# An encoder trunk on one core: the mLSTM recurrence's products in two groups a head, gate sums by transposes, and the order of the last output turns

## The chip, the cores and the metric

The kernel runs on one core of a Trainium2 chip. The metric is the device time of one execution in microseconds (us); less is better. Before the change it is 2804.45 us, the median of three runs from 2801.84 to 2805.65.

The engines' names in the profile: PE is TensorE (matrix products; PEld is its weight loads), DVE is VectorE, ACT is ScalarE, POOL is GpSimd, and SP is SyncE, which issues the DMAs. PSUM is the memory that PE writes its sums to. It has eight banks of 128 partitions x 512 float32 values, and the kernel hands them out one by one.

## What is computed

One layer of a hybrid encoder on 2048 tokens of width 1024, in float32. The part that the change touches is the mLSTM: 4 heads of 128 features, each with a 128 x 128 matrix memory that is carried from chunk to chunk. Cut to what matters (the input gate and forget gate come from eight columns of the input projection; `w`, `dw`, `s_prev` and `inter` are exponentials of gate sums):

```python
proj = rms_norm(x) @ w_in                        # q, k, v, mq, mk, mv, mo, i, f, ga, gm
att = chunk_band_attention(q, k, v, rel_bias)    # 8 heads, own chunk and 8 before it
# mLSTM, for each chunk and head:
c_loc = einsum('lv,lk->vk', w * v, k)
c_new = s_prev * c_prev + s_loc * c_loc          # state before the chunk: c_prev, n_prev
num = inter * (c_prev @ q) + (qk * dw) @ v
den = inter * (n_prev @ q) + sum(qk * dw)
hout = num / maximum(abs(den), exp(-m))
# then a norm for each head, gates, projections:
x = x + (sigmoid(ga) * (att @ w_att_proj) + sigmoid(gm) * (mlstm @ w_mlstm_proj)) @ w_out
x = x + square(relu(rms_norm(x) @ w_up)) @ w_down
out = rms_norm(x)
```

## The kernel before

The 2048 tokens are four blocks of 512. The kernel works on the mLSTM in chunks of 128 tokens, so a block has four chunks. Blocks 0 and 1 are worked one after the other with plain products; blocks 2 and 3 ("far") are taken together by a scheme of seven products in place of eight (`quad`, `quad_tok`, `down`), with intermediate tiles kept in HBM. Large products are made of three products of split operands (high by high, high by low, low by high): `mm3`, lines 531 to 533, and `quad`, line 616. They are the dense work, and the profile shows their 128x512 matmuls on those lines. Small products, the recurrence's and all transposes, are float32 without a split. The planner calls them full products and marks them "pe~"; the profile records each float32 product twice and each transpose once.

**The planner.** The program is a set of threads, Python generators that ask for an engine and a time ("pe~", 660) or for buffers ("get", a pool, how many). `Flow` plays them against a clock of its own when the kernel is built, and the order in which it grants the engines is the order of the instructions. Its latencies (LAT) and the times in the yields are estimates in the code. One thread, `dense`, issues the dense work and has the last priority; the threads of the attention, the recurrence and the evacuations put their PE steps between. A PE step of such a thread is placed SLACK (800 ns) after the time at which the planner expects it to be ready, so that PE finds it ready; NEAR (150) holds instead where PE is already at full products. SWITCH (85) is charged to the first product behind full ones that isn't full itself. A thread gets PSUM banks only if `want` banks less those that the dense work holds stay free for the dense work.

**The gates** (`gates`, from line 1354). The gate columns' product lands in a bank as 40 rows of 512 tokens, the low part's sums in rows 32 to 39 and the high part's in rows 0 to 7. ACT copies it to tmp. Four products (line 1368), one for 128 tokens each, with the 40 x 8 matrix sel, turn it and add the two parts. DVE adds the bias: in block 0 with a scale, four instructions (line 1374), in the others one (line 1378). `gates_rest` makes the exponentials of it.

**The recurrence** (`rec_head`, from line 1605). For each block and head: w gets the decay weights, kt the turned and weighted keys, then w the weighted scores. Then the loop over the four chunks takes one bank a chunk and puts three float32 products into it: scores by values (line 1654), weighted keys by values (1655), queries by the state cst (1656). DVE makes the next state (1659) from cst and the second product, and the next chunk's third product reads it. `rec_out` (from line 1711) scales the third product on ACT (1714), adds the first on DVE (1716), frees the bank, and sums squares (1720). Behind the loop, the head's output is normed, turned (1691) and multiplied by its output gate (1695). There are 4 blocks of 4 heads, so 64 rounds of the loop. In blocks 0 and 1 several heads are under way at once; in blocks 2 and 3 one at a time (N_REC).

**The end** (`final`). The norm of the last block needs a sum over the features of squares. `final1` squares each tile of features; the last one's square goes its own way (line 2310). `final_scale` adds them up with products by ones (lines 2393 and, for the last tile, 2400), DVE takes the means (2404) and POOL the root (2408). `final_out` turns the tiles (2426), four of 128x128 for each token tile t and half g of the features, scales them on ACT (2437) or DVE (2439) and stores 128 x 512 values (2443). A thread of it waits for its four tiles to be scaled before it turns them, and for the root before it scales.

Of the kernel before, what the change touches and what calls it, by code (L numbers as in the profile page):

```python
# [27 lines left out]
ALU = mybir.AluOpType  # L28

P = 128  # L30
# [4 lines left out]
NT = T // P  # L35
KT = D // P
AH, AD = 8, 64
MH = 4
# [57 lines left out]
class Flow:  # L96
# [141 lines left out]
class Layer:  # L238
# [1115 lines left out]
    def gates(self, b, bk, less=None):  # L1354
        fl, nc, B, sm = self.fl, self.nc, self.blk[b], self.sm
        V = nc.vector
        if b == 1:
            yield "wait", self.blk[0]["mix_ev"][4:]
        (tmp,) = yield "get", self.temp, 1
        yield "act", act_ns(512, True)  # L1360
        nc.scalar.copy(tmp[:40, :512], bk[:40])
        if less is not None:
            yield "dve", dve_ns(512)
            V.tensor_sub(tmp[:40, :512], tmp[:40, :512], less[:40])
            fl.put(self.banks, less)
        yield "pe~", 756
        for c in range(NT):
            nc.tensor.matmul(bk[:, c * 8:c * 8 + 8], tmp[:40, c * P:(c + 1) * P], self.sel[:40],
                             start=True, stop=True)
        gf = self.gf[b % 2]  # L1370
        if b == 0:
            for c in range(NT):
                yield "dve", 85
                V.scalar_tensor_tensor(gf[:, c], bk[:, c * 8:c * 8 + 8], self.rr["x"][:, c:c + 1],
                                       self.bif[:, c], op0=ALU.mult, op1=ALU.add)
        else:
            yield "dve", 85
            V.tensor_add(gf, bk[:, :32].rearrange("p (a b) -> p a b", a=NT), self.bif)
# [226 lines left out]
    def rec_head(self, b, h):  # L1605
# [42 lines left out]
        nev = [Event() for _ in range(NT)]  # L1648
        for c in range(NT):
            n = c * MH + h  # L1650
            sl = slice(c * P, (c + 1) * P)
            (bk,) = yield "get", self.banks, 1
            yield "pe~", 660
            mm(bk[:, 0:129], w[:, sl], mv[c], start=True, stop=True)  # L1654
            mm(bk[:, 130:259], kt[:, sl], mv[c], start=True, stop=True)  # L1655
            mm(bk[:, 260:389], q[:, sl], cst, start=True, stop=True)  # L1656
            fl.spawn(self.rec_out(n, bk, ndv[:, c], hs, c, nev[c]), 1)
            yield "dve", 265
            V.scalar_tensor_tensor(cst, cst, ex[:, 3, n:n + 1], bk[:, 130:259], op0=ALU.mult, op1=ALU.add)
        yield "wait", nev  # L1660
        den = ndv[:, :, 128]
        exh = ex[:, 0].rearrange("p (c m) -> p c m", c=NT)[:, :, h]
# [45 lines left out]
            fl.put(self.rec_room, 0)  # L1708
        fl.set(B["mix_ev"][4 + h])

    def rec_out(self, n, bk, nd, hs, c, ev):
        fl, nc = self.fl, self.nc
        yield "act", act_ns(129, True, 1)
        nc.scalar.mul(nd, bk[:, 260:389], self.ex[:, 1, n:n + 1])
        yield "dve", dve_ns(129)
        nc.vector.tensor_add(nd, bk[:, 0:129], nd)
        fl.put(self.banks, bk)
# [667 lines left out]
    def final_scale(self, s, h, slot, summed, ready):  # L2385
# [9 lines left out]
        if last:  # L2395
            fl.put(self.bias, slot)
            yield "wait", [self.last_ev]
            yield "pe~", 900
            for t in range(NT):
                nc.tensor.matmul(bk[:, 2 * t:2 * t + 2], self.sq_last[:, t * P:(t + 1) * P], self.ones,  # L2400
                                 start=False, stop=True, skip_group_check=True)
        r = self.rr[f"z{h}"]
        yield "dve", 75
        nc.vector.tensor_scalar(r, bk[:, :2 * NT].rearrange("p (t a) -> p t a", a=2)[:, :, 0], 1.0 / D, None,
# [15 lines left out]
    def final_out(self, s, h, t, g, scaled, ready, sent):  # L2420
        fl, nc = self.fl, self.nc
        yield "wait", scaled
        (bk,) = yield "get", self.banks, 1
        yield "pe~", 107 * 4
        for i in range(4):
# [8 lines left out]
        e = yield "act|dve", 650  # L2434
        r = self.rr[f"z{h}"][:, t:t + 1]
        if e == "act":
            nc.scalar.mul(o[:, :512], bk, r)
        else:
            nc.vector.tensor_scalar(o[:, :512], bk, r, None, op0=ALU.mult)
        fl.put(self.banks, bk)  # L2440
        row = (2 * s + h) * T + t * P
        yield "sp", 900, 2000
        nc.sync.dma_start(self.io["out"][row:row + P, g * 512:g * 512 + 512], o[:, :512])
        fl.put(pool, slot)
        fl.set(sent)

# [4 lines left out]
    def build(self):  # L2451
# [25 lines left out]
        self.last_ev, self.ev_late, self.ev_r, self.ev_gain, self.ev_const = (Event() for _ in range(5))  # L2477
# [129 lines left out]
```

## Time and profile before

| what | value |
|---|---|
| time, median of three runs | 2804.45 us |
| the profiled execution's own time | 2800.38 us |
| its span, first to last instruction | 2798.6 us |
| granted PE clock, mean | 0.999 |
| PE busy | 2776.0 us |
| DVE busy | 2069.1 us |
| ACT busy | 1563.4 us |
| HBM traffic | 437.46 MB read, 179.31 MB written |

How to read it: the profile is of one execution, with times from the start of the span. A row of the groups gives line, engine, operation, tiles (out<-in), shapes and count, then busy time and the mean ns of one, then the engine's idle time just before them and what ended it. A matmul's end is modelled, and matmuls overlap: the distance from one start to the next says what one costs. A row of the timeline has start, length, the instruction and how many were merged; the idle time before it stands in brackets. A row of the waits has who waited for whom, then us in total, times, and the longest. A row of the windows has the stretch, its length, the busy time of each engine that is named in its heading, and at the end the granted clock, the DMA engines' busy share and GB/s.

### The profile page before, as it was taken

The page shows a single profiled execution, that of the slowest core. Times are in us where ns is not written, and L with a number is a line of the kernel's source. Part 1 is how long each engine was busy: PE and PEld are TensorE (multiplying, and loading weights), DVE is VectorE, ACT ScalarE, POOL GpSimd, SP SyncE. Part 2 cuts the span into 40 slices and gives each one's busy share as a digit, 9 for nine tenths or more (in the row PEclk, how much of TensorE's full clock was granted, in tenths as well). Part 3 has the DMA queues.
Part 4 walks back from the last instruction along what each step waited for, and adds up shares of the span by engine and source line. Part 5 has one row for each costly group of instructions (what it writes and reads, how often), then busy time and mean ns, then how long its engine had stood idle before and what let it go on. Part 6 is the DMA issues. An engine that isn't in the chain of part 4 may idle for free.

```text
span 2798.6 us, 38177 instructions
## 1 busy us (share of the span) xinstructions
PE 2776.0 (99%) x13100; PEld 2300.7 (82%) x13100; DVE 2069.1 (74%) x3827; ACT 1563.4 (56%) x2707; POOL 50.5 (2%) x116
## 2 busy tenths in 40 slices
PE   9999999999999999999999999999999999999998
PEld 7888888888878888888888888888888888888887
DVE  7986489958885976875777888789877564457675
ACT  5774366755453544585555776466544665554443
POOL 0000000000000000000000000000000000000000
PEclk9999999999999999999999999999999999999999
DMA  6326742267845689657878876867777475677773
GB/s 223 102 90 211 266 147 90 97 209 240 268 154 201 230 289 311 218 199 256 305 286 296 279 242 210 254 193 231 236 253 238 171 255 206 208 268 263 266 260 130
DMA packets 283634, 619.33 MB, mean 221 GB/s; under 512 B 31536, under 2 KB 46000, under 8 KB 283440
## 3 DMA queue, kind: packets, MB, share of 16 engines
q1 hardware_dynamic: 283296, 616.88, 65.7%
q8 instruction: 103, 1.69, 0.2%
q14 instruction: 91, 0.75, 0.1%
q10 hardware_dynamic: 144, 0.01, 0.0%
HBM read 437.46 MB, written 179.31 MB: 220 GB/s over the span
## 4 chain that ended last, share of the span: by engine, by line
PE 90%; DVE 5%; issue 2%; ACT 2%; DMA 1%; POOL 0%; SPq 0%; POOLq 0%; DVEq 0%; ACTq 0%
PE bank L616 40%; PE bank L531 13%; PE bank L532 12%; PE bank L533 12%; PE bank L644 3%; PE bank L1272 2%; PE bank L1310 2%; PE bank L1344 2%; DVE wsp L472 1%; PE bank L1654 0%; PE bank L1636 0%; PE bank L1656 0%; PE bank L1655 0%; ACT wsp L470 0%; DVE r L1349 0%
## 5 line engine op out<-in xcount | busy, mean ns | idle before, releaser
L616 PE MATMUL bank<-r,wsp 128*128 128x512 f32 x5208 | 1188.6, 390 | 0.9 <-DVE r L1022 0.7
L616 PEld LDWEIGHTS bank<-r,wsp 128*128 128x128 f32 x5208 | 976.3, 188 | 208.4 <-issue 1.9
L472 DVE TENSOR_TENSOR wsp<-wraw,wsp 128x1024 fp32r<-128x1024 f32 x460 | 562.4, 1223 | 309.5 <-ACT wsp L470 301.0
L470 ACT CAST wsp<-wraw 128x1024 fp32r<-128x1024 f32 x460 | 483.0, 1050 | 493.6 <-PE bank L616 246.6
L531 PE MATMUL bank<-r,wsp 128*128 128x512 f32 x1600 | 636.0, 398 | 2.2 <-DVE ctx L1695 1.5
L532 PE MATMUL bank<-r,wsp 128*128 128x512 f32 x1600 | 625.2, 391 | 0.0
L533 PE MATMUL bank<-r,wsp 128*128 128x512 f32 x1600 | 624.8, 391 | 0.0
L533 PEld LDWEIGHTS bank<-r,wsp 128*128 128x128 f32 x1600 | 300.4, 188 | 64.2
L531 PEld LDWEIGHTS bank<-r,wsp 128*128 128x128 f32 x1600 | 300.6, 188 | 59.0 <-DVE ctx L1695 1.9
L532 PEld LDWEIGHTS bank<-r,wsp 128*128 128x128 f32 x1600 | 301.1, 188 | 55.2 <-DVE r L1294 0.8
L1848 DVE TENSOR_TENSOR ctx<-bank,ctx 128x512 f32<-128x512 f32 x174 | 119.4, 689 | 101.8 <-PE bank L616 101.7
L1020 DVE TENSOR_TENSOR r<-r 128x512 fp32r<-128x512 f32 x224 | 149.2, 688 | 61.1 <-ACT r L1015 60.1
L1015 ACT CAST r<-r 128x512 fp32r<-128x512 f32 x224 | 135.3, 621 | 94.2 <-DMA r<-u 91.1
L1840 ACT COPY ctx<-bank 128x512 f32<-128x512 f32 x174 | 100.9, 582 | 75.7 <-PE bank L616 67.7
L1325 ACT ACTIVATE sc<-sc,scs 128x640 f32<-128x640 f32 (+4 forms) x128 | 97.4, 761 | 62.4 <-DVE scs L1322 58.5
L1316 DVE CUSTOM_DVE_ANT_0 sc<-bank,bias 128x320 f32<-128x320 f32 (+3 forms) x240 | 106.3, 461 | 4.6 <-PE bank L1310 3.6
L2200 ACT ACTIVATE ctx<-ctx 128x512 f32<-128x512 f32 x96 | 60.6, 631 | 84.1 <-DVE ctx L1848 84.0
L1349 DVE TENSOR_TENSOR r<-bank,r 128x512 fp32r<-128x512 f32 (+1 forms) x168 | 97.1, 595 | 10.2 <-ACT r L1347 9.4
L1272 PE MATMUL bank<-r,r 128*128 128x512 f32 x336 | 96.6, 370 | 1.8 <-DVE r L1349 1.4
L1347 ACT CAST r<-bank 128x512 fp32r<-128x512 f32 (+1 forms) x168 | 81.4, 515 | 28.5 <-PE bank L1344 24.7
L1310 PE MATMUL bank<-r,r 128*128 128x320 f32 (+3 forms) x480 | 85.7, 304 | 0.4 <-DVE r L1174 0.3
L1344 PE MATMUL bank<-const,sc 128*128 128x128 f32 x560 | 81.1, 274 | 4.9 <-DVE sc L1330 3.4
(282 smaller groups left out, 2886.2 us busy)
## 6 DMA issues: line engine op xcount, KB each, us to landing
wraw<-in_wf SPq DMA_DIRECT2D x170, 512.0 KB, 4.4
wraw<-wsum SPq DMA_DIRECT2D x136, 512.0 KB, 4.1
r<-u SPq DMA_DIRECT2D x224, 256.0 KB, 4.4
wraw<-in_w SPq DMA_DIRECT2D x103, 512.0 KB, 3.5
u<-ctx SPq DMA_DIRECT2D x128, 256.0 KB, 2.6
ctx<-in_wf SPq DMA_DIRECT2D x112, 256.0 KB, 4.1
wsum<-ctx SPq DMA_DIRECT2D x112, 256.0 KB, 3.6
u<-tmp SPq DMA_DIRECT2D x96, 256.0 KB, 3.2
```

What stands on the lines that cost most here:

```text
L470: nc.scalar.copy(w[:, 0], raw)
L472: nc.vector.tensor_sub(w[:, 1], raw, w[:, 0].bitcast(F32))
L531: mm(ps, lh, rh, start=first, stop=False)
L532: mm(ps, lh, rl, start=False, stop=False)
L533: mm(ps, ll, rh, start=False, stop=last)
L616: mm(ps, wv[:, x, k, n], a[:, y], start=new and k == 0 and x == y == 0, stop=k == 3 and x == 1, skip_group_check=True)
L1015: self.nc.scalar.copy(dst[:, 0], src)
L1020: self.nc.vector.tensor_sub(dst[:, 1], src, dst[:, 0].bitcast(F32))
L1272: nc.tensor.matmul(bkv[:, :, c0:c0 + w], st, sl[:, :, o:o + w], start=n == 0, stop=n == total - 1)
L1310: nc.tensor.matmul(bks[x][:, :w], q[:, y, i * P:(i + 1) * P], kf[:, f * P + x * w:f * P + x * w + w], start=y == 0, stop=y == 1)
L1344: nc.tensor.transpose(bk[:, o:o + P], prob[i][0][:, c:c + P], self.ident)
L1848: nc.vector.tensor_add(t[:, o:o + 512], ps, t[:, o:o + 512])
```

## The change

It has five parts. SLACK goes from 800 to 720. The gate sums are turned by four transposes of 40 columns, and DVE adds the two parts together with the bias, in two rounds. The recurrence's products come in two groups: first all four of weighted keys by values and the first two of scores by values, in two banks (own and late); then three state updates in a row, which leave the states before chunks 1, 2 and 3 in kt, in the place of the weighted keys that have been used; then the other two of scores by values and the four of queries by states, in two more banks (rest and far). The last update writes cst. late, rest and far are freed when all four outputs have been read. At the end, the output's transposes wait for the last sums to be issued, but for those of half 1 of the first two token tiles; and the first token tile is scaled and stored in two pieces of 256 columns. Cut to its core:

```diff
-    SLACK = 800.0
+    SLACK = 720.0
...
-        yield "pe~", 756
+        yield "pe~", 436
         for c in range(NT):
-            nc.tensor.matmul(bk[:, c * 8:c * 8 + 8], tmp[:40, c * P:(c + 1) * P], self.sel[:40],
-                             start=True, stop=True)
+            nc.tensor.transpose(bk[:, c * 40:c * 40 + 40], tmp[:40, c * P:(c + 1) * P], self.ident[:40, :40])
         gf = self.gf[b % 2]
+        gv = bk[:, :160].rearrange("p (a b) -> p a b", a=NT)
         if b == 0:
-            for c in range(NT):
-                yield "dve", 85
-                V.scalar_tensor_tensor(gf[:, c], bk[:, c * 8:c * 8 + 8], self.rr["x"][:, c:c + 1],
-                                       self.bif[:, c], op0=ALU.mult, op1=ALU.add)
+            for n in (0, 32):
+                for c in range(NT):
+                    yield "dve", 85
+                    V.scalar_tensor_tensor(gf[:, c], gv[:, c, n:n + 8], self.rr["x"][:, c:c + 1],
+                                           (gf if n else self.bif)[:, c], op0=ALU.mult, op1=ALU.add)
         else:
-            yield "dve", 85
-            V.tensor_add(gf, bk[:, :32].rearrange("p (a b) -> p a b", a=NT), self.bif)
+            for n in (0, 32):
+                yield "dve", 100
+                V.tensor_add(gf, gv[:, :, n:n + 8], gf if n else self.bif)
...
-        for c in range(NT):
-            n = c * MH + h
-            sl = slice(c * P, (c + 1) * P)
-            (bk,) = yield "get", self.banks, 1
-            yield "pe~", 660
-            mm(bk[:, 0:129], w[:, sl], mv[c], start=True, stop=True)
-            mm(bk[:, 130:259], kt[:, sl], mv[c], start=True, stop=True)
-            mm(bk[:, 260:389], q[:, sl], cst, start=True, stop=True)
-            fl.spawn(self.rec_out(n, bk, ndv[:, c], hs, c, nev[c]), 1)
-            yield "dve", 265
-            V.scalar_tensor_tensor(cst, cst, ex[:, 3, n:n + 1], bk[:, 130:259], op0=ALU.mult, op1=ALU.add)
+        own, late = yield "get", self.banks, 2
+        yield "pe~", 1330
+        for c in range(NT):
+            mm(*((own, late)[c // 3][:, col[c % 3]], kt[:, sl[c]], mv[c]), start=True, stop=True)
+        for c in range(2):
+            mm(late[:, col[1 + c]], w[:, sl[c]], mv[c], start=True, stop=True)
+        state = [cst] + [kt[:, col[c]] for c in range(3)]
+        for c in range(3):
+            yield "dve", 265
+            V.scalar_tensor_tensor(state[c + 1], state[c], ex[:, 3, c * MH + h:c * MH + h + 1], own[:, col[c]],
+                                   op0=ALU.mult, op1=ALU.add)
+        fl.put(self.banks, own)
+        rest, far = yield "get", self.banks, 2
+        yield "pe~", 1330
+        mm(rest[:, col[2]], q[:, sl[0]], cst, start=True, stop=True)
+        for c in range(2, NT):
+            mm(rest[:, col[c - 2]], w[:, sl[c]], mv[c], start=True, stop=True)
+        for c in range(1, NT):
+            mm(far[:, col[c - 1]], q[:, sl[c]], state[c], start=True, stop=True)
+        for c in range(NT):
+            fl.spawn(self.rec_out(c * MH + h, late[:, col[1 + c]] if c < 2 else rest[:, col[c - 2]],
+                                  far[:, col[c - 1]] if c else rest[:, col[2]], ndv[:, c], hs, c, nev[c], read[c]), 1)
+        yield "dve", 265
+        n = 3 * MH + h
+        V.scalar_tensor_tensor(cst, state[3], ex[:, 3, n:n + 1], late[:, col[0]], op0=ALU.mult, op1=ALU.add)
+        yield "wait", read
+        fl.put(self.banks, late, rest, far)
         yield "wait", nev
...
             for t in range(NT):
                 nc.tensor.matmul(bk[:, 2 * t:2 * t + 2], self.sq_last[:, t * P:(t + 1) * P], self.ones,
                                  start=False, stop=True, skip_group_check=True)
+            fl.set(self.sums_ev)
...
         yield "wait", scaled
+        if g == 0 or t > 1:
+            yield "wait", [self.sums_ev]
         (bk,) = yield "get", self.banks, 1
...
+        n = 256 if t == 0 else 512
+        for c in range(0, 512, n):
+            e = yield "act|dve", 40 + 1.2 * n
+            if e == "act":
+                nc.scalar.mul(o[:, c:c + n], bk[:, c:c + n], r)
+            else:
+                nc.vector.tensor_scalar(o[:, c:c + n], bk[:, c:c + n], r, None, op0=ALU.mult)
+            if c + n == 512:
+                fl.put(self.banks, bk)
+            yield "sp", 1.76 * n, 2000
+            nc.sync.dma_start(self.io["out"][row:row + P, g * 512 + c:g * 512 + c + n], o[:, c:c + n])
```

In `rec_out` only the operands' names change (own and far in place of columns of one bank), and it sets the event read instead of freeing the bank.

More of the change, by code (lines that the diff above doesn't have):

```diff
@@ new lines, in rec_head @@
+        sl = [slice(c * P, (c + 1) * P) for c in range(NT)]
+        col = [slice(129 * c, 129 * c + 129) for c in range(3)]
+        own, late = yield "get", self.banks, 2
+        yield "pe~", 1330
+        for c in range(NT):
+            mm(*((own, late)[c // 3][:, col[c % 3]], kt[:, sl[c]], mv[c]), start=True, stop=True)
[3 more added lines that the diff above has]
+        for c in range(3):
+            yield "dve", 265
+            V.scalar_tensor_tensor(state[c + 1], state[c], ex[:, 3, c * MH + h:c * MH + h + 1], own[:, col[c]],
+                                   op0=ALU.mult, op1=ALU.add)
@@ L1709, in rec_head, with rec_out @@
         fl.set(B["mix_ev"][4 + h])
-    def rec_out(self, n, bk, nd, hs, c, ev):
+    def rec_out(self, n, own, far, nd, hs, c, ev, read):
         fl, nc = self.fl, self.nc
         yield "act", act_ns(129, True, 1)
-        nc.scalar.mul(nd, bk[:, 260:389], self.ex[:, 1, n:n + 1])
+        nc.scalar.mul(nd, far, self.ex[:, 1, n:n + 1])
         yield "dve", dve_ns(129)
-        nc.vector.tensor_add(nd, bk[:, 0:129], nd)
-        fl.put(self.banks, bk)
+        nc.vector.tensor_add(nd, own, nd)
+        fl.set(read)
         (tmp,) = yield "get", self.temp, 1
@@ L2476, in build @@
         self.x_sent, self.w_sent = E(KT), E(KT // 2)
-        self.last_ev, self.ev_late, self.ev_r, self.ev_gain, self.ev_const = (Event() for _ in range(5))
+        self.last_ev, self.sums_ev, self.ev_late, self.ev_r, self.ev_gain, self.ev_const = (Event() for _ in range(6))
         self.u_ev = [[[E(4) for _ in range(7)] for _ in range(4)] for _ in range(NS)]
```

10 lines of the change are left out of this document (1 added, 9 removed).

## The prediction

> **What bounds the kernel now.** I read the page's head, its clock row and its chain first.
>
> ```profile
> span 2798.6 us, 38177 instructions
> PE 2776.0 (99%) x13100; PEld 2300.7 (82%) x13100; DVE 2069.1 (74%) x3827; ACT 1563.4 (56%) x2707; POOL 50.5 (2%) x116
> PEclk9999999999999999999999999999999999999999
> PE 90%; DVE 5%; issue 2%; ACT 2%; DMA 1%; POOL 0%; SPq 0%; POOLq 0%; DVEq 0%; ACTq 0%
> ```
>
> TensorE (PE) is busy for 2776.0 of 2798.6 us, at nine tenths or more of its clock in every slice, and it makes up 90% of the chain. So a change can help in two ways only: fewer or cheaper PE instructions, or less of the 22.6 us in which PE is idle. Where those lie, the timeline of PE at both ends and the view of waits say:
>
> ```profile
> 0.94 4.02 PE L296 MATMUL bank<-ones 128*128 128x128 f32 x20 [0.94 <-DVE ones L291]
> 5.45 1.19 PE L531 MATMUL bank<-wsp,r 128*128 128x512 f32 x4 [0.49 <-ACT wsp L453]
> 2788.90 0.98 PE L2426 MATMUL bank<-const,ctx 128*128 128x128 f32 x7 [0.16 <-DVE r_z L2404]
> ```
>
> ```profile
> PE bank L1344 <- DVE sc L1330: 3.4, 5, 1.1
> PE bank L531 <- DVE ctx L1695: 1.5, 1, 1.5
> PE bank L1272 <- DVE r L1349: 1.4, 3, 0.8
> ...
> PE bank L2426 <- DVE r_z L2404: 0.2, 1, 0.2
> ```
>
> PE's last transposes end at 2788.90 + 0.98 = 2789.88, so 2798.6 - 2789.88 = 8.7 us are the tail behind PE. The start takes 0.94 + 0.49 = 1.4 us, and one wait of 0.16 lies in the tail. There remain 22.6 - 8.7 - 1.4 - 0.2 = 12.3 us of waits in the whole middle, in small pieces: the view has fifteen rows with 23 waits in all, and the longest single one is 1.5 us. None of its rows names the recurrence's state (L1659) or its output (L1716) as what PE waited for.
>
> **The recurrence in two steps.** Per head, 12 float32 products were issued in four groups of three; after the change they come in two groups of six, with the same operands.
>
> ```profile
> L1654 PE MATMUL bank<-ctx,ctx 128*128 128x129 f32 x128 | 25.1, 277 | 0.8 <-issue 0.8
> 108.83 0.38 PE L1654 MATMUL bank<-ctx,ctx 128*128 128x129 f32 x2
> 109.05 0.39 PE L1655 MATMUL bank<-ctx,ctx 128*128 128x129 f32 x2
> 109.27 0.39 PE L1656 MATMUL bank<-cst,ctx 128*128 128x129 f32 x2
> 109.42 0.48 PE L531 MATMUL bank<-r,wsp 128*128 128x512 f32 x1
> 109.73 0.39 PE L532 MATMUL bank<-r,wsp 128*128 128x512 f32 x1
> 109.96 0.39 PE L533 MATMUL bank<-r,wsp 128*128 128x512 f32 x1
> ```
>
> L1654 stands for 64 products (16 heads of 4 chunks) and has 128 records: each float32 product is two. The starts show a product every 0.22 us, so 0.11 a record, and a dense product every 0.23. What does a change between the two kinds cost? The planner's SWITCH charges 85 ns for the first dense product behind float32 ones. The rows show the dense L531 at 109.42, only 0.15 behind the start of a product that should take 0.22, and the next one 0.31 later instead of 0.23: the 0.08 that comes late was gained just before. From 108.83 to 109.73 are 0.90 us, and three products and one dense one make 3 x 0.22 + 0.23 = 0.89. So a group costs about 0.01 us beyond its work; 64 groups become 32. That is 32 x 0.01 = 0.3 us; the other ends are nothing and, by SWITCH, 32 x 0.085 = 2.7 us. I take 0.4, near the row.
>
> The DVE and ACT instructions of the recurrence are the same in number. Their waits change:
>
> ```profile
> L1659 DVE SCALAR_TENSOR_TENSOR cst<-cst,g_ex,bank 128x129 f32<-128x129 f32 x64 | 22.2, 347 | 13.2 <-PE bank L1656 8.6 <-ACT ctx L1714 4.0
> L1714 ACT ACTIVATE ctx<-bank,g_ex 128x129 f32<-128x129 f32 x64 | 23.5, 367 | 25.2 <-PE bank L1656 14.9 <-DVE cst L1659 9.9
> ```
>
> L1659 and L1714 read the same bank and stand in each other's way (4.0 and 9.9 us). In the new order the state updates read own and late, and the scaling reads rest and far, so these 13.9 us of idle DVE and ACT go. Neither engine bounds the kernel, so I count nothing. What is new is a chain: the second group waits for three updates of 0.35 us one behind the other, 1.05 us with nothing of this head on PE. Dense products and the attention's lie in that time, as they now lie between the four groups. If that cover were missing, it would cost 16 x 1.05 = 17 us; the planner puts the group SLACK behind the last update, so it isn't missing. Queued behind the waiting PE group is the dense stream itself, so an update that comes late by more than the slack is paid in full.
>
> **The gate sums, turned.** Four blocks each have four products with a 40 x 8 operand; each becomes one transpose.
>
> ```profile
> 837.38 1.06 PE L1368 MATMUL bank<-sel,tmp 40*128 40x8 f32 x8
> 838.36 0.88 PE L1398 MATMUL bank<-r,gw 128*40 128x512 f32 x3
> 429.55 0.60 PE L1691 MATMUL bank<-const,ctx 128*128 128x128 f32 x4
> 429.98 0.82 PE L1344 MATMUL bank<-const,sc 128*128 128x128 f32 x6
> L1374 DVE SCALAR_TENSOR_TENSOR g_gf<-bank,r_x,bif 128x8 f32<-128x8 f32 x4 | 0.7, 221 | 4.6 <-PE bank L1368 4.6
> L1378 DVE TENSOR_TENSOR g_gf<-bank,bif 128x32 f32<-128x32 f32 x3 | 0.6, 192 | 6.0 <-PE bank L1368 6.0
> ```
>
> Eight records took 838.36 - 837.38 = 0.98 us, four transposes elsewhere 429.98 - 429.55 = 0.43. A transpose is one record of 0.11, so 0.44 to 0.55 us a block go; the lower value holds if what the 40-row operand costs at the group's edges stays. Four blocks at 0.47 make 1.9 us. The ends: nothing, if a transpose of 40 columns took as long as a product, and 2.2. The two halves are now added by DVE: four more of L1374 (0.9 us) and three more of L1378 (0.6 us). They lie beside dense products, with the rest of the gate chain behind them and the recurrence only later; uncovered they would cost 1.5 us.
>
> **The end.** The output's transposes of half 0, and of half 1 for the last two token tiles, now wait until the last sums are issued; the stores of the first token tile are cut in two.
>
> ```profile
> 2780.02 1.47 PE L2426 MATMUL bank<-const,ctx 128*128 128x128 f32 x12
> 2785.46 0.60 PE L2426 MATMUL bank<-const,ctx 128*128 128x128 f32 x4
> 2786.39 0.63 ACT L2310 ACTIVATE tmp<-ctx 128x512 f32<-128x512 f32 x1 [1.35 <-DVE ctx L2264]
> 2786.71 1.07 PE L2426 MATMUL bank<-const,ctx 128*128 128x128 f32 x8
> 2787.62 0.95 PE L2400 MATMUL bank<-ones,tmp 128*128 128x2 f32 x8
> 2788.92 1.01 POOL L2408 TENSOR_TENSOR r_z<-r_z,half 128x4 f32<-128x4 f32 x1 [32.28 <-DVE r_z L2404]
> 2790.68 0.33 SPq L2443 DMA_DIRECT2D out_x<-wraw  x1
> 2791.10 0.88 SPq L2443 DMA_DIRECT2D out_x<-sc  x2
> 2794.54 0.59 SPq L2443 DMA_DIRECT2D out_x<-wraw  x1
> 2792.00:2793.00 1.00, 0.00 (x0) 0.00 (x0) 0.69 (x2) 0.38 (x1) 0.00 (x0) 0.93 1.03 383
> 2796.00:2797.00 1.00, 0.00 (x0) 0.00 (x0) 0.00 (x0) 0.00 (x0) 0.00 (x0) 0.50 1.00 377
> DMA to landing us min/median/max: 2.1/2.8/3.0
> ```
>
> The squares that the last sums (L2400) read are there at 2786.39 + 0.63 = 2787.02, but eight transposes hold PE until 2787.62. With none there the sums start some 0.5 us earlier. Of the 12 transposes at 2780.02, which lie ahead of the last dense products, only eight may stay: 4 x 0.11 = 0.4 us. The 24 that move behind the sums take 2.6 us on an idle PE, beside the 1.01 us of L2408 and the scaling. Each of the six tiles takes 0.44 and two are done beforehand, so they stay ahead of a scaling that needs two engines 2.4 us or more for eight. From then on the DMA engines are full, at 383 and 377 GB/s in the windows: 2 MB in some 5.5 us. Cutting the first stores lets data flow some 0.3 us sooner, but adds two issues at about 0.45 (the two at 2791.10 take 0.88), with half the data behind each of the first four. I count zero, between -0.3 and +0.9. The end: -0.9 us.
>
> Here a rule speaks against the change. The Trainium skill, "DMA: Bandwidth & Descriptors", Anatomy of one DMA, gives a DMA (one issued from GpSimd, while these are SP's) a fixed 2.0 us plus its bytes at 436 GB/s. By it, as an estimate, 256 KB are 2.6 us, and eight strung together 20.8; two halves more would add 4.0. This trace doesn't agree that they add up: eight stores take 2794.54 - 2790.68 = 3.86 us to issue and at most 3.0 more to land, 6.9 in all.
>
> **SLACK.** The planner now places a step of the non-dense threads 80 ns closer to when it expects it to be ready. Every one of the 23 waits can grow by 0.08, 1.8 us at most; but one stall puts PE back for the next ones too. I take +0.2. It also moves every later decision of the planner, so that the middle's 12.3 us are dealt anew. I know no sign for that.
>
> The sum: -0.4 - 1.9 - 0.9 + 0.2 = **-3.0 us**. The profiled execution took 2800.38 us, 1.8 more than its span; it would take 2797.4. It lies 4.07 below the median of the three runs shown (2804.45, from 2801.84 to 2805.65), and I take the difference to the median: **2801.45 us**. A measurement of this kernel can tell about 0.2%, 5.6 us, from no change.
>
> **The rivals.**
> - *The new order also removes waits.* Heads that finish sooner and less blocking between DVE and ACT let the late items of the view of waits arrive in time. For it: the worst rows are DVE being late (L1330, L1349), and DVE loses 4.0 us of idle time. Against it: those rows are the attention's, not the recurrence's. If half of the 12.3 us goes, it is -3.0 - 6.1 = -9.1: 2795.3. Chance 0.31.
> - *PSUM banks run short (slower).* A head held one bank per chunk, each until its output was added; now late is held across both steps, and rest and far with it: three of eight, while the dense work reserves two to four. From the point at which the reserve is all that is free, attention's threads queue, or a dense sum waits for a bank that a head reads. That second kind is in the trace once: L531 waited 1.5 us for L1695, which reads such a bank. Were it to come once in each of eight of the 16 heads, it is 8 x 1.5 = 12 us: -3.0 + 12 = +9, 2813.5. Against it: four held banks a head, one after another, become two shorter stays. Chance 0.13.
> - *The groups don't come together.* If float32 groups already lie beside the attention's transposes, which are float32 too, halving them saves nothing, and the rest gives -2.6: 2801.85. Chance 0.08.
> - *Each added store pays its whole way.* Two more stores, each with the least time to landing of the row above, 2.1 us, make +4.2 - 3.0 = +1.2: 2805.65. By the page named above it would be 4.0, and the trace bears out neither. Chance 0.03.
> - *The forecast*, 2801.45 within a few us: 0.45.
>
> **How the numbers follow.** Forecast, third and fourth rival lie within 0.2%: 0.45 + 0.08 + 0.03 = 0.56. Faster by more 0.31, slower by more 0.13. The forecast's own range, from the ends of its terms and the 3.8 us between runs, is 2797 to 2806. The whole range takes in the first rival and a part of the second: 2794 to 2809.
>
> **What would show it.** Right: L1368 with 16 records instead of 32 and PE some 2 us less busy; six float32 products in a row in each of 32 groups, still 0.11 us a record; the last sums about 0.1 us behind their square; the view of waits with about 12 us again, on other rows. Wrong: new PE waits on L1695, on the state updates or on a bank; transposes of 40 columns slower than 0.11; DMA below 380 GB/s in the tail; middle waits under 8 or over 17 us.

## The result, and the profile after

The changed kernel takes 2805.41 us (median of 21 runs, 2804.09 to 2807.59) against 2801.84 us for the kernel before in the same rounds (21 runs, 2799.21 to 2805.65). The ratio is 1.0013 with a 95% interval of 1.0007 to 1.0019: 3.6 us slower, 0.13%. That lies inside the 0.2% and inside the range, but on the other side of no change than the forecast. The forecast's time, 2801.45 us, is 4.0 us off only because it started from the median of three runs, 2804.45, and the 21 runs put the kernel before 2.6 us lower; as a difference, -3.0 was forecast and +3.6 came.

The page of the changed kernel, its head and the engines of its chain:

```profile
span 2805.6 us, 38177 instructions
PE 2777.7 (99%) x13084; PEld 2303.1 (82%) x13084; DVE 2071.4 (74%) x3832; ACT 1562.5 (56%) x2711; POOL 49.2 (2%) x116
PE 89%; DVE 6%; issue 2%; ACT 1%; DMA 1%; POOL 0%; POOLq 0%; ACTq 0%; SPq 0%; DVEq 0%
```

PE has 16 records fewer, as the gates' transposes should make it, and yet is busy 1.7 us longer, and it is idle for 2805.6 - 2777.7 = 27.9 us instead of 22.6. This profiled execution is the slowest of its 21, so the two profiles differ by 7.0 us of span where the medians differ by 3.6: the profiles show where the time lies, the medians how much it is.

The view of waits of the changed kernel (who waited for whom, then us in total, times, longest):

```profile
PE bank L1714 <- DVE ctx L1703: 4.0, 4, 1.8
PE bank L1628 <- DVE scs L1316: 2.6, 2, 2.4
PE bank L1344 <- DVE sc L1330: 2.1, 5, 0.8
PE bank L1344 <- DVE scs L1316: 1.4, 2, 0.8
PE bank L1639 <- DVE scs L1316: 1.2, 1, 1.2
PE bank L531 <- DVE scs L1316: 1.1, 1, 1.1
```

L1316 is the DVE instruction that reads the attention's score banks. Before the change it was in no row of what PE waited for; now four rows name it, 6.3 us together. L1628, L1639 and L531 read nothing that it writes, so what they wait for is a PSUM bank that the scores still occupy. Where is that? All kernels here issue 10392 products on the lines of the dense work, in the same order but for a few dozen places (21 in the changed kernel), so the same product's start can be compared from kernel to kernel. Between the gates and 1500 us the two kernels keep step (the changed one is 0.2 us ahead at 1500), from 1500 to 2060 it loses 6.2 us, and behind that 1.0. The stretch from 1500 to 2060 is the far blocks', in which the down projection runs beside the attention and the recurrence of blocks 2 and 3. The timeline of PE in the changed kernel shows what happens there:

```profile
1731.37 0.40 PE L533 MATMUL bank<-r,wsp 128*128 128x512 f32 x1
...
1735.75 0.66 PE L1628 MATMUL bank<-const,r 128*128 128x128 f32 x4 [2.36 <-DVE scs L1316]
...
1737.29 0.33 PE L1344 MATMUL bank<-const,sc 128*128 128x128 f32 x1 [0.58 <-DVE scs L1316]
1738.78 1.22 PE L1639 MATMUL bank<-r 128*128 128x128 f32 x4 [1.16 <-DVE scs L1316]
1739.79 1.70 PE L1344 MATMUL bank<-const,sc 128*128 128x128 f32 x7
...
1750.45 0.39 PE L531 MATMUL bank<-r,wsp 128*128 128x512 f32 x1
```

No dense product starts for 1750.45 - 1731.37 = 19.1 us. By the code, the dense thread stands at `project(2)` (line 806) there, which waits for all eight parts of block 2's mix, the attention's among them. What is left for PE are small products of the late attention and recurrence, each behind a DVE or ACT step. The dense stream had run ahead: against before, it was 4.7 us early at 1700 us, and at 1780 it is 11.6 late. Of the kernel before, the windows of the line L531 alone (length, then PE busy with L531, its weight loads, granted clock, DMA share, GB/s) over the same stretch and over a later one:

```profile
1731.80:1750.20 18.40, 6.96 (x18) 3.38 (x18) 1.00 0.81 264
1999.80:2021.40 21.60, 10.87 (x29) 5.18 (x28) 1.00 0.85 284
```

The same view of the changed kernel:

```profile
1731.80:1750.20 18.40, 0.00 (x0) 0.00 (x0) 0.81 0.54 161
1999.80:2021.40 21.60, 9.29 (x24) 4.41 (x24) 1.00 0.80 255
```

Eighteen dense products against none, and a clock of 0.81. The windows of the changed kernel with all engines (PE, PEld, DVE, ACT, POOL, then the clock) show more:

```profile
1730.60:1734.00 3.40, 2.79 (x17) 2.22 (x15) 2.88 (x7) 3.35 (x6) 0.00 (x0) 1.00 0.53 157
1734.00:1737.40 3.40, 1.08 (x7) 0.73 (x7) 3.40 (x11) 3.40 (x11) 0.00 (x0) 1.00 0.80 200
1737.40:1740.80 3.40, 2.24 (x10) 2.05 (x11) 2.94 (x13) 3.16 (x7) 0.00 (x0) 0.52 0.75 261
1740.80:1744.20 3.40, 3.40 (x18) 3.40 (x17) 2.16 (x6) 1.59 (x5) 0.29 (x2) 0.50 0.46 142
1744.20:1747.60 3.40, 3.40 (x27) 3.24 (x26) 2.17 (x6) 1.49 (x4) 0.00 (x0) 0.98 0.09 36
```

DVE and ACT are full from 1734.0 to 1737.4, PE does 1.08 us of work, and then its clock is halved for 6.8 us: seven turns at 1739.79 start 1.50 us before the next instruction, 0.21 each in place of 0.11. So a stop is paid twice. PE is idle in the stage for 10.1 us against 6.4, and 6.8 us at half clock cost at most 3.4; 3.7 + 3.4 = 7.1 for the 6.2 that are missing.

### The profile page after: what moved, and what is told of

Same layout as the page of the kernel before. It is cut to its first block, busy times and chain, and to the rows that moved or that the text cites. A ratio compares the mean times of both kernels' runs of the same rounds, so it can differ in the third digit from the quotient of the medians.

```text
span 2805.6 us, 38177 instructions
## 1 busy us (share of the span) xinstructions
PE 2777.7 (99%) x13084; PEld 2303.1 (82%) x13084; DVE 2071.4 (74%) x3832; ACT 1562.5 (56%) x2711; POOL 49.2 (2%) x116
## 4 chain that ended last, share of the span: by engine, by line
PE 89%; DVE 6%; issue 2%; ACT 1%; DMA 1%; POOL 0%; POOLq 0%; ACTq 0%; SPq 0%; DVEq 0%
PE bank L616 42%; PE bank L531 12%; PE bank L532 12%; PE bank L533 12%; PE bank L644 3%; PE bank L1272 2%; PE bank L1310 2%; PE bank L1344 2%; DVE wsp L472 1%; DVE sc L1316 1%; DVE ctx L1588 1%; DVE r L1349 1%; PE bank L1639 0%; ACT wsp L470 0%; DMA r<-u 0%
## 5 line engine op out<-in xcount | busy, mean ns | idle before, releaser
L531 PE MATMUL bank<-r,wsp 128*128 128x512 f32 x1600 | 635.2, 397 | 1.1 <-DVE scs L1316 1.1
L531 PEld LDWEIGHTS bank<-r,wsp 128*128 128x128 f32 x1600 | 300.6, 188 | 59.0 <-DVE scs L1316 1.8
L1316 DVE CUSTOM_DVE_ANT_0 sc<-bank,bias 128x320 f32<-128x320 f32 (+3 forms) x240 | 105.1, 460 | 5.2 <-PE bank L1310 4.4
L1347 ACT CAST r<-bank 128x512 fp32r<-128x512 f32 (+1 forms) x168 | 80.3, 515 | 26.5 <-PE bank L1344 23.9
L415 DVE TENSOR_TENSOR ctx<-ctx,ctx 128x512 f32<-128x512 f32 x112 | 76.4, 686 | 13.9 <-DMA wsum<-ctx 13.0
```

Of the source, the lines that this page charges most:

```text
L531: mm(ps, lh, rh, start=first, stop=False)
L1316: nc.vector.tensor_tensor_reduce(out=e[:, x * w:x * w + w], in0=bks[x][:, :w], in1=br[:, j0 + x * w:j0 + x * w + w], op0=ALU.add, op1=ALU. ...
```

## The experiments

All edits are made on the kernel before unless said, and each was timed in five rounds against it. The theories: **banks** (a head of the new recurrence holds three of the eight PSUM banks at once, the far stage's dense sums four; `scores` asks for two banks in one request, so the attention is held up until the dense stream catches up with it), **blocks** (six float32 products in one PE step, 1.33 us, delay others), **slack** (80 ns less slack expose waits), **deal** (any edit deals the planner's order anew, and the time lands some us to either side), and later **amount** (the time for which banks are held counts, not the number at once) against **threshold** (the number at once counts). Part by part first.

**SLACK alone** (`SLACK = 800.0` to `720.0`).

> The kernel before with SLACK 720 alone. Bank theory (the new recurrence takes three to four PSUM banks a head, and PE then waits for banks that DVE's L1316 still reads): no new PE wait on L1316, time within 1.5 us of before. Slack theory (steps placed 80 ns sooner find their data late): the wait rows of PE grow by 3 to 6 us in the middle and the time is 3 to 5 us above before. Deal theory (any edit re-deals the planner's order in the stages with attention, and the sum of PE's waits there lands anywhere within some 5 us): a difference of either sign of 1 to 5 us, with the waits on other rows, and no L1316 rule.

Measured: 2801.43 against 2800.27 us, ratio 1.0006 (0.9997 to 1.0014). It can't be told from nothing, and, as its interval reaches 3.9 us, not from the whole loss either; the run of all but the recurrence, below, decides that. Its profile has a stop of 11.5 us at full clock.

**The recurrence alone** (the diff's part in `rec_head` and `rec_out`, SLACK 800).

> The kernel before with the recurrence in two steps alone, SLACK 800. Bank theory: new PE waits on L1316 of 4 us or more, the stage of the far attention (some 1530 to 2040 us) longer by 4 to 7 us, the time 4 to 6 us above before. Slack theory: within 1.5 us of before, at best 1 us below. Deal theory: either sign, 1 to 5 us; waits on L1316 may come or not.

Measured: 2821.02 against 2800.27, ratio 1.0075 (1.0063 to 1.0088), 20.7 us slower, much more than the whole change and than the 4 to 6 us that banks had said. In its far stage the dense stream stops twice, from 1734.3 for 20.0 us and from 1999.6 for 22.1. The windows of L531 alone:

```profile
1734.80:1754.20 19.40, 0.00 (x0) 0.00 (x0) 0.82 0.48 153
2000.00:2021.60 21.60, 0.00 (x0) 0.32 (x1) 0.78 0.51 169
```

and from its view of waits the row that leads it:

```profile
PE bank L1344 <- ACT sc L1332: 11.3, 5, 4.3
```

L1344 turns the attention's probabilities and L1332 scales them. All five of these waits lie in the two stops: PE has nothing else left to do. No row says that PE waited for a state update. The waits on L1316 that banks had expected, 4 us or more, are 0.8 us here.

**All but SLACK** (the changed kernel with `SLACK = 800.0`) and **all but the recurrence** (SLACK, gates and end, with the old loop).

> The changed kernel with SLACK put back to 800. Bank theory: PE still waits on L1316 for 4 us or more; the time stays within 1.5 us of the changed kernel, some 3 us above before. Slack theory: the loss goes, and the gates' 2.5 us remain as a gain: 2 to 4 us below before. Deal theory: anything between 4 us below and 5 us above before, not the sum of the parts.

> The changed kernel with the old recurrence loop (SLACK 720, turned gate sums, new order at the end). Bank theory: no PE wait on L1316, time 2 to 4 us below before. Slack theory: 0 to 3 us above before, as the changed kernel nearly. Deal theory: either sign by some us, and the far stage differs from e1's though only gates and end differ.

Measured: 2818.80, ratio 1.0067 (1.0053 to 1.0080), with stops of 20.1 and 22.9 us; and 2797.74, ratio 0.9995 (0.9986 to 1.0003). None of the theories had the 18.5 us of the first. So the loss is the recurrence's: without it the other parts aren't slower than before (its one stop, of 11.5 us, is at full clock). And the 80 ns of slack, worth nothing that can be told alone, take 15 us off it. That is what made the change look small.

**The gates alone** (the diff's part in `gates`).

> The kernel before with the turned gate sums alone. By the profiles so far each of the four gate steps is 0.6 us shorter, so 2.5 us less on PE; the banks' theories give 2 to 3 us below before, since nothing in the far blocks changes. Deal theory: some us to either side.

Measured: 2795.72 against 2800.35, ratio 0.9985 (0.9977 to 0.9994): 4.6 us faster, with an interval from 1.7 to 6.4. This version beats both kernels. The gates' four places are worth 2.4 us of it (below), which lies inside the interval. Its profile has 21.3 us of idle PE for before's 22.6; whether more than the 2.4 is real, and comes from an order dealt anew, isn't shown.

**One more bank** (the old loop with a bank that nothing uses; **two** of them in the next).

```diff
+        (spare,) = yield "get", self.banks, 1
         for c in range(NT):
...
         yield "wait", nev
+        fl.put(self.banks, spare)
```

> The kernel before (SLACK 800, old loop), but each head holds one more PSUM bank, unused, from ahead of its loop until its four outputs are done. Bank theory, by amount (the two steps cost 20 us because a head holds more bank time while the dense work leaves four of eight banks): PE idle comes ahead of the two projections of the far blocks (near 1745 and 2010 us) and the time is 8 us or more above before. Block theory (what costs is two steps of 1.33 us that ask for two banks at once and then three updates in a row, whatever they hold): within 3 us of before. Deal theory (the planner's order is dealt anew by any edit): either of these, unrelated to the other runs.

> The kernel before (SLACK 800, old loop), but each head holds two unused PSUM banks over its loop, so that a head has three banks or more at once, as with late, rest and far. Threshold theory (with four banks held by the dense sums, a head with three leaves one, and the attention's scores ask for two at once; one spare bank left them two): the dense stream stops ahead of both far projections for 15 us or more each, and the time is 15 us or more above before. Amount theory, refuted in part by the one spare bank that cost nothing, gives 0 to 8 us. Deal theory: within 5 us of before, as one spare bank.

Measured: with one, 2799.77 against 2799.74, ratio 1.0000 (0.9991 to 1.0009). With two, 2824.37 against 2800.35, ratio 1.0084 (1.0070 to 1.0098), 24.0 us slower, with not one instruction of the kernel different in kind. The windows of L531 alone, with one bank:

```profile
1720.00:1760.00 40.00, 12.21 (x32) 5.77 (x31) 1.00 0.68 214
1990.00:2030.00 40.00, 19.75 (x51) 9.40 (x51) 1.00 0.68 227
```

and with two:

```profile
1720.00:1760.00 40.00, 1.27 (x3) 0.56 (x3) 0.83 0.36 106
1990.00:2030.00 40.00, 15.84 (x40) 7.38 (x40) 1.00 0.64 218
```

With one spare there is one stop of 8.8 us at full clock, which costs nothing in the median; with two the dense stream stops for 50.4 us. This shows the banks' effect without any part of the change, and that the first spare bank is free and the second is not. It also speaks against amount: in the planner's own play (whose times are estimates in the code, not the chip's) the far heads hold 266 us of bank time before the change, 368 with one spare bank, 362 with late held (below) and 394 in the recurrence alone. The 368 cost nothing, the 362 cost 15.2 us. In the same play a head has three banks or more for 2 us before, 14 with one spare, 41 with late held, 54 in the recurrence alone and 95 with two spare, which goes roughly with the losses at SLACK 800. It doesn't give the price at a smaller slack: 45 us in the changed kernel come with 3.6 us of loss.

**Late freed early** (two steps, SLACK 800). The first step takes the first chunk's query product along, so that late can be freed while the second step is under way (`rec_last` makes the last update, waits until the first chunk's output has been read, and frees late); then **late held**, which keeps late until all four outputs have been read, with the line that this diff takes out last, and is the same otherwise.

```diff
-        for c in range(2):
-            mm(late[:, col[1 + c]], w[:, sl[c]], mv[c], start=True, stop=True)
+        mm(late[:, col[1]], q[:, sl[0]], cst, start=True, stop=True)
+        mm(late[:, col[2]], w[:, sl[0]], mv[0], start=True, stop=True)
+        fl.spawn(self.rec_out(h, late[:, col[2]], late[:, col[1]], ndv[:, 0], hs, 0, nev[0], read[0]), 1)
...
+        fl.spawn(self.rec_last(3 * MH + h, cst, state[3], late, late[:, col[0]], read[:1]), 1)
...
-        fl.put(self.banks, late, rest, far)
+        fl.put(self.banks, rest, far)
```

> The two steps at SLACK 800, but the first step also holds chunk 0's other two products (scores by values, queries by state) in late in place of the scores by values of chunks 0 and 1, so that late is freed before the second step is under way; the same 12 products a head in two groups of six. Bank theory: most of the 20 us goes, within 4 us of before. Block theory: the same two blocks and pairs of banks, so 15 to 20 us above before. Deal theory: anywhere between.

> The two steps with late freed early, but late is kept until all four outputs have been read: the products, their order and their steps are the same, and only the time of freeing differs (SLACK 800). Threshold theory: the dense stream stops ahead of the second projection too, and the time is 8 us or more above the version that frees late early (2803.9). Order theory (what helped was the products' new order, which lets chunk 0's output go first): within 3 us of that version. Deal theory: anywhere between.

Measured: freed early, 2803.88 against 2799.74, ratio 1.0014 (1.0005 to 1.0023), 4.1 us slower; held, 2815.58 against 2800.35, ratio 1.0055 (1.0043 to 1.0068), 15.2 slower. The products, their groups and their updates are the same in both. The windows of L531 with late freed early:

```profile
1720.00:1760.00 40.00, 10.81 (x25) 4.98 (x25) 0.87 0.53 164
1990.00:2030.00 40.00, 22.27 (x57) 10.70 (x57) 1.00 0.83 280
```

and held:

```profile
1720.00:1760.00 40.00, 10.20 (x25) 4.78 (x25) 0.91 0.58 184
1990.00:2030.00 40.00, 11.60 (x29) 5.65 (x30) 0.87 0.55 179
```

The second stretch has 57 dense products with late freed early and 29 with late held: the second stop, which the recurrence alone has at 1999.6, is back, 11.6 us long. The first stop is in both, 12.1 us with late freed early and 11.5 with late held, and both have half clock behind it: freeing late early doesn't take that one away.

**The steps cut** (two steps, SLACK 800, each PE step asked for in two halves; the banks are held as in the recurrence alone).

```diff
-        yield "pe~", 1330
-        for c in range(NT):
-            mm(*((own, late)[c // 3][:, col[c % 3]], kt[:, sl[c]], mv[c]), start=True, stop=True)
+        yield "pe~", 665
+        for c in range(3):
+            mm(own[:, col[c]], kt[:, sl[c]], mv[c], start=True, stop=True)
+        yield "pe~", 665
+        mm(late[:, col[0]], kt[:, sl[3]], mv[3], start=True, stop=True)
```

> The two steps at SLACK 800 with the same banks and holds, but each PE step asked for in two halves of three products, so that the planner may put other work between. Bank theory: the holds stay or grow, 15 us or more above before. Block theory: most of the loss goes, within 5 us of before. Deal theory: anywhere between.

Measured: 2817.00 against 2799.74, ratio 1.0062 (1.0050 to 1.0075), 17.3 us slower, with a stop of 31.0 us. The trace has 59 of the 64 groups of three products apart. The steps are half as long and most of the loss stays: blocks falls.

**Both cures together** (the changed kernel with late freed early), and **less slack still** (the recurrence alone with `SLACK = 640.0`).

> The changed kernel (SLACK 720, gates and end as changed) with the first step of the run before last, late freed early. Bank theory: 2 to 6 us below before, since the loss of the recurrence goes and the gates' 2.5 us stay. Block theory: no better than the changed kernel, some 4 us above before. Deal theory: anywhere between.

> The two steps alone at SLACK 640 in place of 800. Threshold theory (a bank is taken before the step is placed, so SLACK is part of each hold, and a smaller one gives banks back sooner): 8 us or more below the two steps at 800 (2821.0), and still some us above before. Slack theory as in the prediction (steps that are placed sooner find their data late): no better than at 800. Deal theory: anywhere between.

Measured: 2805.60 against 2799.74, ratio 1.0021 (1.0012 to 1.0030), 5.9 us slower where I expected a gain; and 2804.77 against 2800.35, ratio 1.0017 (1.0008 to 1.0026), 4.4 slower. The second came as threshold had it: a bank is taken before its PE step is placed, so the slack is a part of every hold, and less of it frees the bank earlier. But that this is how the smaller slack helps isn't shown: in the planner's play the time with three banks or more is 51 us at SLACK 640 and 54 at 800, nearly the same. The first is a miss: two edits that each take most of the loss away do not add up. With late freed early, a head of this kernel has three banks for 7 us in the play where the changed kernel has them for 45, and it is no faster.

The stages of the profiled executions, from the starts of the same dense products, against before's (1500.0, 560.1 and 538.4 us; span 2798.6):

| kernel | up to 1500 | 1500 to 2060 | behind | PE idle, 1500 to 2060 | at half clock there |
|---|---|---|---|---|---|
| before | 0 | 0 | 0 | 6.4 | 0 |
| after | -0.2 | +6.2 | +1.0 | 10.1 | 6.8 |
| SLACK alone | 0.0 | +2.1 | 0.0 | 8.9 | 0 |
| recurrence alone | +2.5 | +18.6 | -0.1 | 18.5 | 17.1 |
| all but SLACK | +1.0 | +18.9 | +1.2 | 19.8 | 17.1 |
| all but the recurrence | -3.4 | +1.5 | -0.3 | 8.4 | 0 |
| gates alone | -3.1 | -0.6 | +0.2 | 5.9 | 0 |
| one spare bank | -2.5 | +2.6 | 0.0 | 8.4 | 0 |
| two spare banks | -0.1 | +24.9 | 0.0 | 21.0 | 20.5 |
| late freed early | +1.1 | -0.2 | +3.1 | 6.0 | 10.2 |
| late held | +1.3 | +13.1 | +0.2 | 15.0 | 17.1 |
| steps cut | -0.5 | +15.8 | +0.6 | 12.9 | 23.9 |
| late early, all | -5.0 | +5.2 | +4.9 | 10.3 | 6.8 |
| SLACK 640 | -1.8 | +6.8 | 0.0 | 11.5 | 3.4 |

Every large loss lies in the middle column, and only the kernels with the new loop or with two spare banks have half clock there. The added idle time and half of the time at half clock make up the loss within 0.9 us for the changed kernel, two spare banks and SLACK 640. In the other kernels with half clock they are more than the loss, by 2 to 5 us, so half of that time is the most that it costs: with late freed early, 10.2 us at half clock come with no loss in the stage at all.

## Why the prediction was wrong in sign

**The failed step** is the one that costed the recurrence's new order at 0.4 us of gain and set its banks aside: "four held banks a head, one after another, become two shorter stays". Alone, at SLACK 800, that order costs 20.7 us, and within the change some 6 (+3.6 us with it, -2.5 without). What counts at SLACK 800 is the number of banks at once, three for long in place of one or two: two spare banks cost 24.0 us in the old loop, and freeing late early takes 11 of the 15.2 us of late held off. In the changed kernel itself, at SLACK 720, freeing late early brought nothing, so there the banks as the cause are argued, not shown. The rival *PSUM banks run short* had the holder and the number (three of eight) right, and was given 0.13. Its price was worked from the wrong place: a dense sum that waits for a bank, 1.5 us at a time. Such waits did come, the 6.3 us on L1316, but with the recurrence alone, which loses 20.7 us, they make up 0.8. The attention waits for banks in the planner's order, which no view shows, and the bill comes later, where the dense stream has run ahead to a point that needs the attention. That the attention's requests are what is held up is read from the code and the planner's play; that banks held at once make the long stops is shown, at SLACK 800.

**The three updates in a row** are hidden, as predicted: L1674 waited 0.2 us for L1665 in the whole run. The mutual waits of L1659 and L1714, 13.9 us on engines that don't bound, went too, and brought nothing.

**The groups.** Predicted -0.4. The timeline of the changed kernel shows them:

```profile
103.35 1.05 PE L1659 MATMUL bank<-ctx,ctx 128*128 128x129 f32 x8
104.24 0.61 PE L1661 MATMUL bank<-ctx,ctx 128*128 128x129 f32 x4
104.61 0.48 PE L531 MATMUL bank<-r,wsp 128*128 128x512 f32 x1
104.92 0.39 PE L532 MATMUL bank<-r,wsp 128*128 128x512 f32 x1
```

Twelve records and the dense product behind them take 104.92 - 103.35 = 1.57 us. Over the run it is 1.572 (median of 14 places); six records and a dense product took 0.900 before (median of 30), and a dense product is 0.227. So a group saved is 2 x 0.900 - 0.227 - 1.572 = 0.001 us, nothing. The groups did come together (30 of the 32 stand unbroken in the trace), but the price was that of the rival in which they don't: nothing.

**The gates.** Predicted -1.9. The group after has 16 records, four at a place; its row, and one place in the timeline:

```profile
L1368 PE MATMUL bank<-const,tmp 40*128 40x40 f32 x16 | 1.8, 235 | 0.0
838.44 0.44 PE L1368 MATMUL bank<-const,tmp 40*128 40x40 f32 x4
838.81 0.66 PE L1401 MATMUL bank<-r,gw 128*40 128x512 f32 x2
```

From a group's first record to the next instruction were 0.98 us at each of the four places, and are 0.37: 4 x 0.61 = 2.4 us. The term was right and a little low: it took a record of 0.11 for each transpose, and they start every 0.06 to 0.08 us. DVE's seven more instructions are in no wait of PE.

**The end.** Predicted -0.9. The timeline of PE in the changed kernel:

```profile
2792.12 0.39 PE L533 MATMUL bank<-r,wsp 128*128 128x512 f32 x1
2792.35 0.95 PE L2416 MATMUL bank<-ones,bias 128*128 128x2 f32 x8
2793.16 1.51 PE L2452 MATMUL bank<-const,ctx 128*128 128x128 f32 x12
2794.50 0.95 PE L2423 MATMUL bank<-ones,tmp 128*128 128x2 f32 x8
2795.32 1.56 PE L2452 MATMUL bank<-const,ctx 128*128 128x128 f32 x12
```

and ACT's square that the last sums read:

```profile
2793.28 0.63 ACT L2333 ACTIVATE tmp<-ctx 128x512 f32<-128x512 f32 x1 [1.34 <-DVE ctx L2287]
```

The square is there at 2793.91 and the sums start at 2794.50, 0.59 behind it, where the forecast said 0.1. Twelve turns still stand ahead of them. By the diff only the eight turns of half 1 of the first two token tiles may come before the last sums, and eight stand ahead of the last dense products; so these twelve are turns that wait for the sums in the planner's order, and they come before them in the program all the same. The order in which the planner grants the engines isn't kept here; why is not shown. The step of the forecast that moved 24 turns behind the sums failed for twelve of them. From the last dense product to the sums are 2.38 us (2794.50 - 2792.12), and in before 2787.62 less 2785.23 makes 2.39. Only the turns ahead of the last dense products are fewer, eight in place of twelve, 0.44 us. Against that stand 13.45 us from the last dense product to the end of the span, before 13.35. The end is worth -0.3, and, with the sums no later behind the dense work than before, the two added stores cost about 0.1, so the rival on stores falls too.

**SLACK.** Predicted +0.2 as a cost of exposed waits; alone it is within its interval of nothing. In the change it is worth 15 us, a path that I hadn't seen; that it works by shortening the banks' holds is argued. A cost of exposed waits may be in it too: the largest row of the waits after, L1714 (the turns of a head's normed output, L1691 before) on L1703, 4.0 us, comes with the old loop as well, 1.6 us with SLACK alone and 3.6 in all but the recurrence, and no kernel at SLACK 800 has more than 1.2 of it.

**The marks.** PE's middle waits are 27.9 - 8.7 (from 2796.88 to the end) - 0.95 (start) = 18.2 us, over the 17 that were to prove the forecast wrong; the sign that was named, new waits on a bank, came with 6.3 us, but the waits in the stops of the recurrence alone are mostly for the attention's own steps.

**What stays open.** With late freed early 4.1 us are still lost, and with all parts 5.9. In the profile of the first, 3.1 of them lie behind the far stage, where `quad` waits 2.0 us for ACT's L1017 (3.0 in the second); I have no experiment that says why it is late. L2437's wait for POOL, 1.1 us in the changed kernel and 0.9 in the one with all parts and late early, is in none of the others and was not followed up. The first stop comes in all of these kernels but before and the gates alone, with the old loop too, and what makes it cost anything at a smaller slack is not shown. Differences of the size of the change's own 3.6 us can also be the deal's, which these runs don't exclude. The end's part alone was not run, and the dense work's reserve of banks was not changed.

## What to carry to other kernels

Count the buffers that a step holds at once, with what others reserve and the largest request that must still fit, before counting its instructions: with four banks reserved out of eight and a request of two, one more bank in the old loop was free and two more cost 24.0 us. Look for such a cost not at the holder's waits but at the next point where the main stream needs what was held up. And try the parts alone: the gates by themselves make 2795.72 us, and the smaller slack had hidden most of what the recurrence costs.

## What the runs showed of the hardware

Float32 transposes of 40 columns start 0.06 to 0.08 us apart, and four of them take 0.37 us to the next instruction; four of 128 columns took 0.43 in the kernel before. A run of twelve float32 records is as dear as two of six: the change of kind between dense and float32 products had no price that could be measured (0.001 us).

TensorE's clock was halved without a long wait. In the changed kernel's windows above, the 3.4 us ahead of the halving have PE busy for 1.08, and no single wait in the stop is longer than 2.36 us; with SLACK 640 it was 1.07 of 3.40. How little work is too little doesn't come out of these runs. With two spare banks the clock was halved behind 3.4 us in which PE did more, and in all but the recurrence it stayed full behind 3.4 us in which PE did less. The windows with all engines, first of two spare banks, then of all but the recurrence:

```profile
1731.80:1735.20 3.40, 1.98 (x10) 1.08 (x8) 3.28 (x19) 2.32 (x6) 0.00 (x0) 1.00 0.62 187
1735.20:1738.60 3.40, 2.50 (x9) 1.76 (x9) 2.77 (x10) 1.52 (x4) 1.02 (x1) 0.50 0.77 217
```

```profile
1996.40:1999.80 3.40, 0.84 (x5) 0.41 (x4) 2.50 (x7) 0.00 (x0) 1.38 (x1) 1.00 0.35 128
1999.80:2003.20 3.40, 3.40 (x17) 2.87 (x18) 3.40 (x6) 0.02 (x1) 0.00 (x0) 1.00 0.24 77
```

The halved pieces in the middle of all runs last 3.4, 6.8 or 10.2 us. The Trainium skill, "TensorE: Matmul & The Clock Gate", Part 1: The HAM clock gate, has the half rate come after an idle window of about 3.4 us that runs freely. The lengths agree; but such a window need not be idle, as the rows show. The same page's "A second HAM failure mode: psum-queue depth-cycling" tells of short idle times between groups that do it too, and the changed kernel's trace agrees with that: its waits ahead of the halving are short, 2.36 us and 0.58.
